# Loading attention keys and queries by halves of the partitions: one transfer of 128 rows becomes two of 64

## The chip, the cores and the metric

The kernel runs on one core of a Trainium2 chip. The core has five engines with instruction streams of their own: TensorE (PE in the profile, with PEld for its weight loads), VectorE (DVE), ScalarE (ACT), GpSimd (POOL) and SyncE (SP), which here only issues transfers. Sixteen DMA engines move data between the off-chip memory and the on-chip buffers. The metric is device time in microseconds (us) of one execution; the time of a kernel is the median of its runs.

## The reference

One layer of a hybrid decoder, for a prompt of 2048 tokens and for 8 sample sequences of 8 tokens. The combined projection feeds two groups of heads: a stick-breaking attention (8 heads of width 64) and a gated DeltaNet (4 heads of width 128). Both outputs go through one output projection and then a gated ConvFFN of width 2816. The part that the change touches is the attention over the prompt:

```python
def sb_block(q, k, v, bias, q_pos, k_pos):
    f32 = jnp.float32
    z = jnp.einsum('bqhd,bkhd->bhqk', q.astype(f32), k.astype(f32)) * (SB_HEAD_DIM ** -0.5)
    z = z + bias.astype(f32)[None, :, None, None]
    mask = k_pos[None, :] < q_pos[:, None]
    log_beta = jax.nn.log_sigmoid(z)
    log_one_minus = jnp.where(mask, jax.nn.log_sigmoid(-z), 0.0)
    later = lax.cumsum(log_one_minus, axis=3, reverse=True) - log_one_minus
    att = jnp.where(mask, jnp.exp(log_beta + later), 0.0)
    out = jnp.einsum('bhqk,bkhd->bqhd', att, v.astype(f32))
    return out.astype(q.dtype)
```

## The kernel before, in words

The program runs through five stages: the modulated norm and the input projection (to about 843 us of the profiled execution), the prompt attention with the DeltaNet recurrence and the sample attention woven into it (843 to about 1716 us), the output projection with the second norm (to about 1962 us), the up-projection with its convolution (to about 2945 us) and the down-projection.

Matmuls get their precision from splitting a number into a rounded part (hi) and a rest (lo). The projection stage writes queries and keys, transposed so that the head dimension is the row, to a buffer `qk_s[2, 2, 512, T]` in the off-chip memory: the first index is query or key, the second is hi or lo, the third is 64 rows for each of the 8 heads, the last is the token.

The attention goes over four pairs of heads `p`, for each over four blocks of 512 query tokens `g`, and inside over the key blocks `c` from `g` down to 0. At the head of a block it loads, all from SP's queue: `ql` (the lo part of both heads' queries, on both halves of the partitions, two transfers of 64 rows, L861), then for each head `e` of the pair a tile `kx` with hi keys in partitions 0 to 63 and lo keys in partitions 64 to 127 (L869) and a tile `q` with the hi queries in both halves (L870), then the values `v` (L874). One matmul then contracts over 128 partitions: (hi keys + lo keys) times hi queries (L892), and a second adds the lo queries (L893). `kx` has nine buffers, `q` four, `ql` two. The tiles are reused from key block to key block, so there are 4 x 4 x 2 = 32 loads of `kx` and as many of `q`, of 128 rows of 2 KB (256 KB) each.

From the scores `z` comes a chain over all engines: a sigmoid on ACT (L894), a mask, one minus it on ACT (L902, L905), the running product on DVE (`P`, L910), a product on DVE, four transposes on PE (`tpa`, L921), a copy on ACT (`aT`, L924) and the matmul with the values on PE (`po`, L929).

Two generators fill the gaps: `delta()`, 17 steps of the recurrence (the function `join` loads `Nm`, L723, and four pieces of `FD`, L727, and inverts a triangular matrix starting at the matmul `qp`, L735; `recur` loads `dT` and `s_`, L777 and L780), and `sample_attention` (the loads `kpg`, L1045, and `vpg`, L1037 and L1046, the matmuls at L1049 to L1091). When the recurrence has ended, the weights of the output projection come in through one buffer `wor` (L1128), split on ACT and DVE into `wo` (L1129, L1130).

The order of the instructions on each engine is not that of the source: a scheduler places the instructions of all engines by its own estimate of their times, once, when the program is built. On the chip each engine then runs its list in that order. SP's list therefore carries loads of all the woven parts, and a row that waits holds up all rows behind it. SP's transfers also take their completion semaphores in turn from a set of eight, and a row waits until the transfer eight rows earlier has landed.

Of the kernel before, what the change touches and what calls it, by code (L numbers as in the profile page):

```python
# [8 lines left out]
F32 = mybir.dt.float32  # L9
# [34 lines left out]
def hybrid_step(  # L44
# [9 lines left out]
    dve, act, pool, pe, sp = nc.vector, nc.scalar, nc.gpsimd, nc.tensor, nc.sync  # L54
# [15 lines left out]
    qk_s = dram.tile([2, 2, 512, T], F32, name="qk_s")  # L70
# [312 lines left out]
    with tc.tile_pool(name="p1a", bufs=1, side="left", reuse_waits="tile") as p1a:  # L383
# [19 lines left out]
        for c2 in range(6):  # L403
            w = split_rows(p1, W[:, 1536 + 256 * c2:1792 + 256 * c2], KD, 256, "w", 10, 6)
            for ci in range(2):
# [3 lines left out]
                for g, (b0, n) in enumerate(GB):  # L409
# [4 lines left out]
                    out = p1a.tile([128, 512], F32, name="dno", tag="dno", bufs=2)  # L414
# [436 lines left out]
    def attention():  # L851
        for p in range(4):
            yield "pair", p
            KS, VS = {}, {}
            for g in range(4):
                gs = slice(512 * g, 512 * g + 512)
# [3 lines left out]
                for x in range(2):  # L860
                    sp.dma_start(out=ql[64 * x:64 * x + 64].bitcast(F32),  # L861
                                 in_=qk_s[0, 1, 128 * p:128 * p + 128, gs].rearrange("(e d) t -> d e t", e=2))
                for e in range(2):
                    h = 2 * p + e
                    hs_ = slice(64 * h, 64 * h + 64)

                    k_ = at_p.tile([128, 512], F32R, name="kx", tag="kx", bufs=9)
                    q = at_p.tile([128, 512], F32R, name="q", tag="q", bufs=4)
                    sp.dma_start(out=k_.bitcast(F32), in_=qk_s[1, :, hs_, gs])  # L869
                    sp.dma_start(out=q.bitcast(F32), in_=qk_s[0, 0, hs_, gs].unsqueeze(0).to_broadcast([2, 64, 512]))  # L870
                    KS[g, e] = k_
                    QS.append(q)
                v = at_p.tile([128, 4, 128], F32, name="v", tag="v", bufs=6)
# [260 lines left out]
    for what, x in attention():  # L1134
        if what == "unit":
            done += 0.55 if x else 1.0
            for f in fill:
                while f[0] is not None and f[2] < f[1] * done / f[3]:
                    f[2] += 1
                    if next(f[0], f) is f:  # L1140
                        f[0] = None
            if fill[0][0] is None and not wos:
                p2.release()
                load_wo("p5wa", 4, 1)
                p5f = tc.alloc_tile_pool(name="p5f", bufs=1, side="left", reuse_waits="tile")
                wpools.append(p5f)
        elif x == 3:
            for f in fill:
                if f[0] is not None:
                    for _ in f[0]:  # L1150
                        pass
            p4.release()
            load_wo("p5wb", 2, 1)
            p5g = tc.alloc_tile_pool(name="p5g", bufs=1, side="left", reuse_waits="tile")
            wpools.append(p5g)
# [458 lines left out]
```

## Time and profile before

| what | value |
|---|---|
| median of 3 runs | 3450.96 us (3447.55 to 3452.15) |
| profiled execution | 3450.76 us, its span 3449.2 us |
| granted TensorE clock, mean | 0.97 |
| PE busy | 3257.8 us, 94% of the span |
| PEld busy | 2749.8 us, 80% |
| DVE busy | 2252.3 us, 65% |
| ACT busy | 1473.0 us, 43% |
| DMA | 460.14 MB, mean 133 GB/s |

The profile's page lists busy time by engine, then the span in 40 slices, the DMA queues, the chain of waits that ended last, and the costliest groups of instructions. A row of the timeline or of the groups names the source line, the engine, and "out<-in" by the names of the tiles; "SPq" is the queue of SP, whose rows are transfers being issued, and their time is that of issuing alone. A row "A <- DMA x" in the list of waits is time that A's engine was idle until a transfer into x had landed. In the table of stretches, "DMA share" is the mean busy share of the sixteen DMA engines.

### The profile page before, as it was taken

To read this page: it belongs to the slowest core of one execution; us is meant where nothing else is said; L and a number is where in the kernel's file an instruction comes from. 1 tells how busy PE (TensorE), PEld (TensorE's weight loads), DVE (VectorE), ACT (ScalarE), POOL (GpSimd) and SP (SyncE) were. 2 spreads that over 40 slices of the span, in tenths; PEclk is the share of its full clock that TensorE was granted. 3 is DMA by queue.
4 is the path that set the end of the run, shared out by engine and by line. 5 is a ranking of instruction groups with operands and counts; after the bars stand their busy time and mean duration, and the time that the engine had idled before them with its cause. 6 is when DMAs were issued, how large, how long until landed. Compare 5 with 4: busy or idle time off the path is not lost.

```text
span 3449.2 us, 54308 instructions
## 1 busy us (share of the span) xinstructions
PE 3257.8 (94%) x19371; PEld 2749.8 (80%) x19371; DVE 2252.3 (65%) x4995; ACT 1473.0 (43%) x3188; POOL 251.8 (7%) x466
## 2 busy tenths in 40 slices
PE   7999999998588998978889999999999999899999
PEld 5968999898355665644578899999999999688887
DVE  5346646876477887879866676666666666656564
ACT  5312336683366785768656632222222222332321
POOL 2000002331011121111100000000000000000000
PEclk9999999999589999989999999999999999999999
DMA  7362239683344555343256532122222222566574
GB/s 238 103 201 83 68 122 276 188 274 95 110 132 126 157 160 159 97 127 105 88 183 193 170 109 69 54 59 59 66 64 60 67 64 63 183 205 205 176 245 132
DMA packets 441996, 460.14 MB, mean 133 GB/s; under 512 B 65543, under 2 KB 343895, under 8 KB 441724
## 3 DMA queue, kind: packets, MB, share of 16 engines
q1 hardware_dynamic: 414012, 411.74, 39.0%
q10 hardware_dynamic: 22080, 28.06, 2.4%
q0 software_dynamic: 5632, 16.86, 1.7%
q8 instruction: 153, 2.51, 0.3%
q14 instruction: 119, 0.97, 0.1%
HBM read 306.56 MB, written 149.97 MB: 132 GB/s over the span
## 4 chain that ended last, share of the span: by engine, by line
PE 81%; DMA 9%; DVE 6%; ACT 2%; issue 2%; SPq 1%; POOL 0%; ACTq 0%; DVEq 0%; POOLq 0%
PE up L229 28%; PE dmm L229 12%; PE fm L229 8%; PE tm L229 7%; PE omm L229 5%; PE po L929 4%; PE tpa L921 3%; PE z L892 2%; DVE P L910 2%; DMA q<-qk_s 2%; PE z L893 1%; DMA wor<-in_w_out_dram 1%; DMA FD<-fd_s 1%; PE mp L204 1%; DMA out_dram<-qkn 1%
## 5 line engine op out<-in xcount | busy, mean ns | idle before, releaser
L229 PE MATMUL up<-sl,wu 128*128 128x424 f32 (+1 forms) x5280 | 1019.2, 355 | 0.0
L229 PEld LDWEIGHTS up<-sl,wu 128*128 128x128 f32 x5280 | 991.0, 188 | 23.9 <-ACT sl L1218 0.4
L229 PE MATMUL dmm<-sl,sl 128*128 128x512 f32 x1848 | 433.3, 395 | 9.5 <-ACT sl L1353 8.3
L229 PEld LDWEIGHTS dmm<-sl,sl 128*128 128x128 f32 x1848 | 347.6, 189 | 94.7 <-ACT sl L1353 11.0
L229 PE MATMUL tm<-w,hh 128*128 128x256 f32 (+1 forms) x2048 | 383.8, 288 | 2.0 <-DVE hh L343 1.4
L910 DVE TENSOR_TENSOR_SCAN P<-P 128x512 f32<-128x512 f32 (+2 forms) x320 | 342.8, 1107 | 44.3 <-ACT P L902 27.3
L229 PEld LDWEIGHTS tm<-w,hh 128*128 128x128 f32 x2048 | 315.1, 190 | 4.0 <-ACT nj L309 1.5
L1428 ACT COPY fpre<-up 128x424 f32<-128x424 f32 (+1 forms) x220 | 110.2, 501 | 481.0 <-PE up L229 481.0
L229 PE MATMUL tm<-w,hl 128*128 128x256 f32 (+1 forms) x1024 | 282.6, 288 | 0.5 <-DVE nr_m L173 0.3
L229 PE MATMUL fm<-hh,w 128*128 128x384 f32 (+2 forms) x960 | 266.9, 357 | 0.0
L894 ACT ACTIVATE sg<-z,bias_b 128x512 f32<-128x512 f32 (+2 forms) x320 | 189.4, 629 | 70.6 <-PE z L893 50.3
L929 PE MATMUL po<-aT,v 128*64 128x512 f32 (+3 forms) x640 | 206.0, 590 | 3.7 <-ACT aT L924 3.7
L924 ACT COPY aT<-tpa 128x512 f32<-128x512 f32 (+1 forms) x320 | 163.9, 529 | 87.4 <-PE tpa L921 64.6
L229 PEld LDWEIGHTS fm<-hh,w 128*128 128x128 f32 x960 | 175.8, 188 | 28.0 <-issue 16.8
L921 PE MATMUL tpa<-ident,sg 128*128 128x128 f32 x1088 | 181.0, 288 | 12.8 <-ACT aT L924 9.9
L921 PEld LDWEIGHTS tpa<-ident,sg 128*128 128x128 f32 x1088 | 128.9, 145 | 79.7 <-issue 33.9
L229 PEld LDWEIGHTS tm<-w,hl 128*128 128x128 f32 x1024 | 188.9, 190 | 1.9 <-DVE hl L344 1.3
L1431 DVE TENSOR_SCALAR fo<-fpre,cwf 128x424 f32<-128x424 f32 (+1 forms) x110 | 47.7, 433 | 214.1 <-ACT fpre L1428 214.1
L892 PE MATMUL z<-kx,q 128*128 128x512 f32 (+2 forms) x320 | 143.9, 451 | 30.1 <-DMA q<-qk_s 26.4
L229 PE MATMUL omm<-wo,mh 128*128 128x512 f32 x512 | 164.2, 400 | 8.0 <-ACT wo L1129 5.1
L229 PE MATMUL fm<-hl,w 128*128 128x384 f32 (+2 forms) x480 | 170.7, 356 | 0.0
L1498 ACT CAST sl<-at 128x1408 fp32r<-128x1408 f32 (+1 forms) x58 | 77.1, 1329 | 202.5 <-PE dmm L229 191.4
(472 smaller groups left out, 5031.2 us busy)
## 6 DMA issues: line engine op xcount, KB each, us to landing
at<-cb_s SPq DMA_DIRECT2D x54, 704.0 KB
wdr<-in_w_down_dram SPq DMA_DIRECT2D x110, 256.0 KB
wada<-in_w_ada_dram SPq DMA_DIRECT2D x48, 512.0 KB
raw<-in_w_up_dram SPq DMA_DIRECT2D x176, 128.0 KB
cb_s<-ff SPq DMA_DIRECT2D x176, 128.0 KB
cb_s<-cb SPq DMA_DIRECT2D x88, 192.0 KB
qk_s<-st SPq DMA_DIRECT2D x128, 128.0 KB
wr<-in_w_in_dram SPq DMA_DIRECT2D x96, 128.0 KB
```

The source lines that it names most:

```text
L204: pe.matmul(mp[32 * c:32 * c + 32, :], lhsT=cT[:, k, :], rhs=wt[:, 512 * c1:512 * c1 + 512], start=(k == 0), stop=(k == KD - 1), tile_posi ...
L229: pe.matmul(out, lhsT=a(k), rhs=b(k), start=(i == 0), stop=(i == 3 * nk - 1))
L892: pe.matmul(z[:, :w], lhsT=QS[e][:, qs_], rhs=KS[c, e][:, :w], start=True, stop=False)
L893: pe.matmul(z[:, :w], lhsT=ql[:, e, qs_], rhs=KS[c, e][:, :w], start=False, stop=True)
L894: act.activation(sg[:, ii, :w], z[:, :w], AF.Sigmoid, bias=bias_b[:, h:h + 1])
L910: dve.tensor_tensor_scan(u, u, u, P[:, ii, w:w + 1], ALU.mult, ALU.bypass)
L921: pe.transpose(tp[:, 128 * i:128 * i + 128], halves[i // 2][:, i % 2, 128 * kb:128 * kb + 128], ident)
L924: act.copy(a_[:, 128 * i0:], tp[:, 128 * i0:])
L929: pe.matmul(po[64 * e:64 * e + 64, c0:], lhsT=VS[c][:, kb, 64 * e:64 * e + 64], rhs=aT[e, kb][:, c0:], start=(diag and kb == 0), stop=(c = ...
L1428: act.copy(pre[:, 2:2 + npr], ps[:, :npr])
L1431: dve.tensor_scalar(out=o[:, :npr], in0=pre[:, 0:npr], scalar1=cwf[:, c, 0:1], scalar2=None, op0=ALU.mult)
L1498: act.copy(ah, raw)
```

## The change

The loads of `kx` and `q` become two transfers each, one for partitions 0 to 63 and one for 64 to 127. For the keys the first half is the hi part and the second the lo part; for the queries both halves read the same hi rows. The bytes, the tiles, the buffers and all arithmetic stay as they were.

```diff
                     k_ = at_p.tile([128, 512], F32R, name="kx", tag="kx", bufs=9)
                     q = at_p.tile([128, 512], F32R, name="q", tag="q", bufs=4)
-                    sp.dma_start(out=k_.bitcast(F32), in_=qk_s[1, :, hs_, gs])
-                    sp.dma_start(out=q.bitcast(F32), in_=qk_s[0, 0, hs_, gs].unsqueeze(0).to_broadcast([2, 64, 512]))
+                    for x in range(2):
+                        sl = slice(64 * x, 64 * x + 64)
+                        sp.dma_start(out=k_[sl].bitcast(F32), in_=qk_s[1, x, hs_, gs])
+                        sp.dma_start(out=q[sl].bitcast(F32), in_=qk_s[0, 0, hs_, gs])
                     KS[g, e] = k_
                     QS.append(q)
```

In the changed program the new transfers stand at L871 and L872, and what stood behind them in the source moves down by two lines. The scheduler, seeing other transfers, also places much of the attention stage in another order, on every engine. Three places on SP's queue show it. The first is the start of the attention: the first block's loads and the first two steps of the recurrence. Before:

```order
L861 DMA ql_10546<-qk_s_60 64x2x512 x2
L869 DMA kx_10549<-qk_s_60 128x1x512
L870 DMA q_10550<-qk_s_60 128x1x512
L869 DMA kx_10553<-qk_s_60 128x1x512
L870 DMA q_10554<-qk_s_60 128x1x512
L874 DMA v_10557<-out_3_dram 128x4x128
L723 DMA Nm_10690<-nm_s_73 128x4x128
L727 DMA FD_10688<-fd_s_74 32x8x32 x4
```

Now:

```order
L861 DMA ql_10546<-qk_s_60 64x2x512 x2
L871 DMA kx_10549<-qk_s_60 64x512
L872 DMA q_10550<-qk_s_60 64x512
L871 DMA kx_10549<-qk_s_60 64x512
L872 DMA q_10550<-qk_s_60 64x512
L871 DMA kx_10555<-qk_s_60 64x512
L872 DMA q_10556<-qk_s_60 64x512
L871 DMA kx_10555<-qk_s_60 64x512
L872 DMA q_10556<-qk_s_60 64x512
L876 DMA v_10561<-out_3_dram 128x4x128
L723 DMA Nm_10694<-nm_s_73 128x4x128
L727 DMA FD_10692<-fd_s_74 32x8x32 x4
```

Here four rows became eight and nothing else moved: `v`, `Nm` and `FD` still stand right behind.

The second place is the third step of the recurrence, where `Nm` and `FD` share the queue with the keys of the fourth query block and the sample attention's first page. Before:

```order
L869 DMA kx_11940<-qk_s_60 128x1x512
L869 DMA kx_11944<-qk_s_60 128x1x512
L1037 DMA vpg_11230<-out_5_dram 8x512
L874 DMA v_11948<-out_3_dram 128x4x128
L723 DMA Nm_11169<-nm_s_73 128x4x128
...
L870 DMA q_11941<-qk_s_60 128x1x512
L940 DMA om_s_67<-ob_10783 128x4x128
...
L869 DMA kx_13037<-qk_s_60 128x1x512
L727 DMA FD_11167<-fd_s_74 32x8x32 x4
```

Now:

```order
L723 DMA Nm_11177<-nm_s_73 128x4x128
L872 DMA q_11292<-qk_s_60 64x512
L871 DMA kx_11297<-qk_s_60 64x512
...
L871 DMA kx_11952<-qk_s_60 64x512
L872 DMA q_11953<-qk_s_60 64x512
L727 DMA FD_11175<-fd_s_74 32x8x32 x4
L871 DMA kx_11952<-qk_s_60 64x512
L872 DMA q_11953<-qk_s_60 64x512
```

`Nm` moved ahead into the loads of the third block, and `FD` stands in the middle of the fourth block's loads, behind the first half of a `q` whose buffer must first come free, and ahead of the sample attention's page, which stood before it.

The third place is where the output projection's weights `wor` come in. Before:

```order
L869 DMA kx_19478<-qk_s_60 128x1x512
L1128 DMA wor_17894<-in_w_out_dram 128x512
...
L1128 DMA wor_17898<-in_w_out_dram 128x512
L870 DMA q_18803<-qk_s_60 128x1x512
L869 DMA kx_19482<-qk_s_60 128x1x512
L1128 DMA wor_17903<-in_w_out_dram 128x512
```

Now:

```order
L871 DMA kx_19140<-qk_s_60 64x512 x2
L849 DMA out_7_dram<-S0_15612 128x8x128
L1130 DMA wor_17942<-in_w_out_dram 128x512
...
L871 DMA kx_19538<-qk_s_60 64x512 x2
L1130 DMA wor_17946<-in_w_out_dram 128x512
L876 DMA v_19550<-out_3_dram 128x4x128
L1130 DMA wor_17951<-in_w_out_dram 128x512
L872 DMA q_18855<-qk_s_60 64x512 x2
```

The weights still alternate with keys and queries; the query load `q_18803`, now in two halves as `q_18855`, stands behind three of them where it stood behind two.

## The prediction

> **What bounds the kernel now.** I read the chain of waits first, since it says which stage can be shortened at all, then the table of stretches over the attention, then the waits of PE and the timeline of SP there.
>
> ```profile
> PE 81%; DMA 9%; DVE 6%; ACT 2%; issue 2%; SPq 1%; POOL 0%; ACTq 0%; DVEq 0%; POOLq 0%
> ...
> core 0: us, PE busy (x) PEld busy (x) DVE busy (x) ACT busy (x) POOL busy (x), PEclk, DMA share, GB/s
> 843.00:960.00 117.00, 55.24 (x330) 37.44 (x329) 41.95 (x82) 33.92 (x76) 6.34 (x31) 0.59 0.36 110
> 960.00:1110.00 150.00, 146.43 (x1107) 95.50 (x1106) 126.28 (x209) 105.29 (x210) 21.19 (x45) 0.94 0.44 126
> 1110.00:1300.00 190.00, 180.25 (x1427) 118.47 (x1425) 160.91 (x249) 138.35 (x286) 39.51 (x73) 0.96 0.52 155
> 1300.00:1345.00 45.00, 33.38 (x279) 22.36 (x278) 30.74 (x64) 24.48 (x60) 3.96 (x21) 0.93 0.57 158
> 1345.00:1490.00 145.00, 141.59 (x1023) 94.09 (x1025) 125.73 (x197) 101.49 (x201) 25.40 (x48) 0.97 0.45 128
> 1490.00:1571.00 81.00, 60.31 (x336) 33.03 (x332) 58.26 (x87) 50.79 (x109) 11.64 (x32) 0.83 0.38 114
> ```
>
> PE ends most of the chain, but 9% of it is waiting for transfers. In the undisturbed stretch from 960 to 1110 us PE is busy 146.4 of 150 us: there TensorE sets the pace, and microseconds that it loses elsewhere in the stage are not caught up. It loses them in three places: 843 to 960 (busy 55 of 117 us, at a clock of 0.59), 1300 to 1345, and 1490 to 1571. What PE waited for, from 843 to 960 (first three rows), from 960 to 1360 (next two) and from 1486 to 1571 (the rest):
>
> ```profile
> PE qp L735 <- DMA FD<-fd_s: 30.1, 2, 28.9
> PE z L892 <- DMA q<-qk_s: 26.4, 3, 12.1
> PE qp L735 <- DMA Nm<-nm_s: 5.2, 1, 5.2
> ...
> PE qp L735 <- DMA FD<-fd_s: 23.5, 3, 10.9
> PE tpp L1049 <- DMA kpg<-in_cache_k_dram: 2.0, 1, 2.0
> ...
> PE tpa L921 <- ACT aT L924: 7.2, 3, 5.8
> PE tpp L1049 <- ACT sgs L1066: 6.9, 1, 6.9
> PE po L929 <- ACT aT L924: 3.7, 1, 3.7
> ```
>
> Only the second row names a tile that the change loads. The others follow from it, which the timeline of SP shows (start, time to issue, row):
>
> ```profile
> 842.67 0.57 SPq L869 DMA_DIRECT2D kx<-qk_s  x1
> 843.36 0.49 SPq L870 DMA_DIRECT2D q<-qk_s  x1
> 843.90 4.75 SPq L869 DMA_DIRECT2D kx<-qk_s  x1
> 848.70 5.48 SPq L870 DMA_DIRECT2D q<-qk_s  x1
> 854.22 5.20 SPq L874 DMA_DIRECT2D v<-out_dram  x1
> 859.52 2.69 SPq L723 DMA_DIRECT2D Nm<-nm_s  x1
> 862.31 5.52 SPq L727 DMA_DIRECT2D FD<-fd_s  x4
> ...
> 921.07 7.14 SPq L869 DMA_DIRECT2D kx<-qk_s  x2
> 928.32 5.19 SPq L1037 DMA_DIRECT2D vpg<-out_dram  x1
> ...
> 944.59 7.48 SPq L727 DMA_DIRECT2D FD<-fd_s  x4
> ```
>
> and two pieces of the chain of waits, whose times run from the issue to the landing:
>
> ```profile
> 843.36 14.16 DMA q<-qk_s
> ...
> 944.59 12.81 DMA FD<-fd_s
> ```
>
> Two transfers of `kx` and `q` go out at 0.5 us each. The third takes 4.75 us to issue, the fourth 5.48, and then even `v`, `Nm` and `FD`, which are other tensors, are held back. The stretches around it say why:
>
> ```profile
> 843.00:845.00 2.00, 2.00 (x19) 2.00 (x19) 0.00 (x0) 0.37 (x1) 0.00 (x0) 1.00 0.91 243
> 850.00:858.00 8.00, 0.34 (x2) 0.38 (x2) 0.00 (x0) 0.00 (x0) 0.00 (x0) 0.55 0.13 48
> ```
>
> From 850 to 858 only `kx` and `q` are in flight: the DMA share is 0.13, which is 2 of 16 engines, and 48 GB/s. A transfer of 256 KB then takes 262144 B / 48 GB/s = 5.46 us, the 5.48 us for which SP hangs. So each of these 64 loads runs on two engines alone, SP's queue is blocked once about two are pending, and all that is queued behind is late. Just before, with `ql`'s two transfers of 64 rows and the first `kx` in flight, the share is 0.91 and the rate 243 GB/s: 64 rows do spread over the engines.
>
> **The change part by part.** It removes 64 issues and adds 128 of half the size.
>
> *The new transfers.* At the rate of the 843 to 845 stretch 128 KB take 131072 / 243 GB/s = 0.54 us; if the halves stayed on two engines, 2.73 us. I take 0.54, because `ql` is the same 64 rows from the same buffer. The issue of one is bounded by these rows (ns, least/median/most):
>
> ```profile
> L1014 SPq DMA_DIRECT2D qsm<-qs_s x1: 503/503/503, 868.6 to 868.6; - x1
> L861 SPq DMA_DIRECT2D ql<-qk_s x32: 585/611/4707, 841.3 to 1577.9; - x32
> L1128 SPq DMA_DIRECT2D wor<-in_w_out_dram x16: 327/342/1376, 1486.7 to 1743.0; - x16
> ```
>
> `qsm` has the very shape of a half (64 rows of 512 numbers): 0.50 us, between 0.34 (`wor`) and 0.61 (`ql`, twice the data). So 128 x 0.50 = 64 us of SP's time stand against 64 x 0.52 = 33 us of unblocked issue before: 31 us more over 860 us, if nothing blocks. In the first block alone the rows from 843.90 to 862.31 take 23.6 us for eight issues that would take 4 unblocked. SP has room, and I charge 5 us for loads that come a few tenths later each (0 to 31).
>
> *843 to 960 us.* PE's waits are 30.1 + 26.4 + 5.2 = 61.7 us. Of the first wait for `q` (12.1 us) some stays: the eight halves are issued from 842.7 at 0.5 us, the first head's four are out by 844.7, and if they land as fast as an undisturbed `wor` does (2.82 us from issue, row below), the matmul starts at 847.0 instead of 843.4 + 14.2 = 857.5. PE was busy until 857.5 - 12.1 = 845.4, so 1.6 us remain. The 28.9 us wait is for an `FD` that was issued at 944.6, behind 7.14 us for `kx`, 5.19 for `vpg` and others; its own issue and landing took 12.8. These go too. But a filling pipeline has waits of its own: undisturbed, 960 to 1110 leaves PE 3.6 us idle in 150, and here the first blocks are short, so I keep 8 us (bounds 2 and 30: the latter if the chain through `qp`, DVE and POOL cannot run faster). Gain 61.7 - 1.6 - 8 = 52. The clock: 330 matmuls in 55.2 us are 167 ns each, against 132 ns in the next stretch, so full clock would give 12 us more; with some idle time left I take 5 (0 to 12).
>
> *960 to 1360 us.* 23.5 + 2.0 = 25.5 us of waits. The last `FD` wait (10.9 us) is this: the chain goes back from the landing, over 5.29 us of transfer, to a queue held by `q` (17.86 us from the start of a blocked `q`):
>
> ```profile
> 1323.10 17.86 DMA q<-qk_s
> 1341.02 5.29 DMA FD<-fd_s
> ...
> 1486.65 8.51 DMA wor<-in_w_out_dram
> ...
> 1504.97 13.68 DMA wor<-in_w_out_dram
> ...
> 1529.41 10.00 DMA wor<-in_w_out_dram
> ...
> 1550.91 2.82 DMA wor<-in_w_out_dram
> ```
>
> The other two waits of that row are alike. I take three quarters: 19 us (10 to 25).
>
> *1486 to 1571 us.* ACT stands at `wo` until `wor` lands and its copies for PE queue behind. Three landings take 8.51, 13.68 and 10.00 us, with `kx` or `q` just ahead of them; the next, alone, takes 2.82. They are late by 32.2 - 8.5 = 23.7 us, of which PE sees 7.2 + 6.9 + 3.7 = 17.8. I take 11 (5 to 17), since the weights still go through one buffer.
>
> Sum: 52 + 5 + 19 + 11 - 5 = 82 us. The profiled execution took 3450.76 us, next to the median of 3450.96; 3450.8 - 82 = 3369 us.
>
> [...]
>
> **The rivals.**
>
> *Something else takes the place (smaller gain).* The recurrence steps form a chain of their own, and the new order puts `FD` behind half a `q` that waits for its buffer. Then only the waits for `q` and `Nm` (26.4 - 1.6 + 5.2 = 30) and the `wor` term (11) go: 41 us, 3410. Against it: those waits end at an `FD` that landed late behind a blocked queue, not at a busy engine. The chance is 0.24.
>
> *All of PE's idle time goes (larger gain).* 61.7 - 1.6 + 12 + 25.5 + 17.8 = 115 us: 3335. It needs a recurrence that never waits, and full clock from the start. The chance is 0.07.
>
> *The halves stay on two engines (the change does not spread them).* The queue is blocked as long as before, the second half of a tile at the same time as the whole was, and 64 more issues at 0.50 us come on top; where SP is blocked they are hidden, elsewhere not: half of 32 us, 3467, slower. It decides as soon as the DMA share under these loads stays near 0.13. `ql` speaks against it. The chance is 0.03.
>
> *Each transfer's fixed part counts (slower).* Of `wor`'s 2.82 us, 2 x 0.54 are data, so 1.74 us are fixed. If SP's queue, with eight transfers pending at most, were bound by that latency, 64 x 1.74 = 111 us would come on top of the gain of 82: 3480. It would need eight pending transfers to take longer to land (2.8 us) than to issue (8 x 0.5 = 4 us), so the rows are against it. [...] The chance is 0.02.
>
> *No change*, by a new order that loses what the loads gain: 0.02.
>
> **How the numbers follow.** The forecast, 3369 us, has a chance of 0.62; alone it spans 3345 to 3395. With the larger part of the smaller-gain case the range is 3340 to 3412, which leaves out the rest of both neighbours and the slow cases. Within 0.2% (7 us) a measurement of this kernel cannot tell a change from none. Faster 0.93, same 0.02, slower 0.05.
>
> **What would show it.** SP's rows for the halves should stay near 0.5 us, with no `v`, `Nm` or `FD` over 3 us for one issue. The DMA share under them should go far above 0.13 in short bursts. PE's waits for `q` should fall from 26.4 to some 2 us and for `FD` before 960 from 30.1 to under 8, the attention should end near 1635 instead of 1716 us, and the stages after it should keep their lengths. Wrong would be: `FD` waits as long as before with a free queue (then the recurrence is the bound), or halves that take 2.7 us each on two engines.

## The result, and the profile after

| | before | changed |
|---|---|---|
| median of 4 runs | 3451.56 us (3447.55 to 3453.89) | 3327.03 us (3320.59 to 3329.44) |
| span of the profiled execution | 3449.2 us | 3324.8 us |

The ratio is 0.9637, with a 95% interval of 0.9621 to 0.9654: the change takes about 125 us off. The forecast was 3369 us with a range of 3340 to 3412, so the direction was right, the gain of 82 us a third too small, and the time below the range. Measured again beside another layout of the buffer ("One transfer of 128 rows again" below), the changed kernel took 3320.0 us against 3449.64 (ratio 0.9626, 0.9613 to 0.9639).

The table of stretches shows where the time went. First the attention as a whole, from the end of the last matmul of the projection to the last matmul with the values, of the kernel before and then of the changed one. The columns are the stretch, its length, the busy time and count of each engine, the granted clock, the DMA share and GB/s:

```profile
845.60:1714.50 868.90, 744.26 (x5355) 471.76 (x5355) 677.51 (x1079) 563.28 (x1150) 131.42 (x305) 0.90 0.42 124
```

```profile
849.90:1596.40 746.50, 716.03 (x5358) 455.71 (x5358) 680.07 (x1086) 564.67 (x1154) 134.40 (x305) 0.98 0.50 146
```

The stage went from 868.9 to 746.5 us, which is 122.4 of the 124.4 us between the two spans. DVE and ACT did the same work in the same busy time; the stages ahead and behind kept their lengths to within 8 us each, and these differences nearly cancel. PE's part splits in two: its idle time fell from 868.9 - 744.3 = 124.6 us to 746.5 - 716.0 = 30.5, a gain of 94, and its busy time fell from 744.3 to 716.0, a gain of 28, for the same matmuls. The clock, 0.90 against 0.98, goes with the second.

The timeline of SP at the start, of the changed kernel, answers to the rows that showed the blocked queue:

```profile
847.04 0.60 SPq L871 DMA_DIRECT2D kx<-qk_s  x1
847.73 0.54 SPq L872 DMA_DIRECT2D q<-qk_s  x1
...
853.77 0.59 SPq L872 DMA_DIRECT2D q<-qk_s  x1
854.41 0.59 SPq L876 DMA_DIRECT2D v<-out_dram  x1
855.10 0.45 SPq L723 DMA_DIRECT2D Nm<-nm_s  x1
855.65 1.93 SPq L727 DMA_DIRECT2D FD<-fd_s  x4
```

None of these rows hangs, though SP stands once, for 2.4 us up to 852.0, until an earlier store has landed. `v` goes out in 0.59 us instead of 5.20, `Nm` in 0.45 instead of 2.69, the four `FD` in 1.93 instead of 5.52. Over all 64 halves of `q` (ns, least/median/most):

```profile
L872 SPq DMA_DIRECT2D q<-qk_s x64: 444/540/1396, 847.7 to 1457.6; - x64
```

Of PE's waits in the attention one for a changed load is left; for `FD` a single wait of 0.4 us remains, further down the list of the changed kernel, whose head is:

```profile
PE tpa L923 <- ACT aT L926: 3.9, 7, 1.4
PE tpt L1085 <- DVE sgs L1076: 3.6, 2, 2.2
PE z L894 <- DMA q<-qk_s: 3.3, 1, 3.3
...
PE qp L735 <- DMA FD<-fd_s: 0.4, 1, 0.4
```

And the first 117 us of the attention, to be read beside the row of 843 to 960 before, and the next stretches:

```profile
849.00:966.00 117.00, 110.20 (x865) 73.73 (x864) 100.66 (x189) 80.65 (x177) 16.16 (x49) 0.90 0.70 190
966.00:1116.00 150.00, 149.78 (x1211) 100.08 (x1209) 137.28 (x224) 116.55 (x243) 25.68 (x62) 1.00 0.54 161
1116.00:1300.00 184.00, 183.96 (x1473) 121.41 (x1475) 164.06 (x259) 139.49 (x288) 35.15 (x77) 1.00 0.53 157
```

PE did 865 matmuls in the time in which it had done 330, and from 966 to 1300 us it idles 0.3 us, at full clock. Most of the idle time that is left lies behind, 23.4 us from 1300 us to the end of the attention.

### The profile page after: what moved, and what is told of

It is laid out like the page before. It is cut to its first block, busy times and chain, and to the rows that moved or that the text cites. A ratio compares the mean times of both kernels' runs of the same rounds, so it can differ in the third digit from the quotient of the medians.

```text
span 3324.8 us, 54372 instructions
## 1 busy us (share of the span) xinstructions
PE 3230.1 (97%) x19371; PEld 2733.8 (82%) x19371; DVE 2250.6 (68%) x4995; ACT 1471.7 (44%) x3188; POOL 255.0 (8%) x466
## 3 DMA queue, kind: packets, MB, share of 16 engines
q1 hardware_dynamic: 415932, 411.75, 40.9%
## 4 chain that ended last, share of the span: by engine, by line
PE 83%; DVE 7%; DMA 6%; ACT 2%; issue 1%; SPq 0%; POOL 0%; ACTq 0%; DVEq 0%; POOLq 0%
PE up L229 28%; PE dmm L229 12%; PE fm L229 8%; PE tm L229 8%; PE omm L229 5%; PE po L931 4%; PE tpa L923 3%; DVE P L912 3%; PE z L894 2%; PE z L895 1%; PE mp L204 1%; DMA raw<-in_w_down_dram 1%; DVE sg L916 1%; DMA nm_s<-Nm 1%; PE tpp L1051 1%
## 5 line engine op out<-in xcount | busy, mean ns | idle before, releaser
L229 PEld LDWEIGHTS up<-sl,wu 128*128 128x128 f32 x5280 | 989.4, 188 | 25.4 <-ACT sl L1220 1.9
L912 DVE TENSOR_TENSOR_SCAN P<-P 128x512 f32<-128x512 f32 (+2 forms) x320 | 343.2, 1108 | 26.4 <-ACT P L907 11.7
L1430 ACT COPY fpre<-up 128x424 f32<-128x424 f32 (+1 forms) x220 | 110.2, 502 | 480.4 <-PE up L229 480.4
L931 PE MATMUL po<-aT,v 128*64 128x512 f32 (+3 forms) x640 | 196.4, 558 | 0.0
```

Source lines behind the costliest of these rows:

```text
L229: pe.matmul(out, lhsT=a(k), rhs=b(k), start=(i == 0), stop=(i == 3 * nk - 1))
L912: dve.tensor_tensor_scan(u, u, u, P[:, ii, w:w + 1], ALU.mult, ALU.bypass)
L931: pe.matmul(po[64 * e:64 * e + 64, c0:], lhsT=VS[c][:, kb, 64 * e:64 * e + 64], rhs=aT[e, kb][:, c0:], start=(diag and kb == 0), stop=(c = ...
L1430: act.copy(pre[:, 2:2 + npr], ps[:, :npr])
```

## The experiments

Theory A: the loads were slow because each ran on two DMA engines, and the gain is their spread over sixteen. Rival B: it is the halving, or the new order of the instructions. Rival C: only the waits of a block's first matmul for its queries count. A further question was where the 28 us of busy time come from.

**The same program with an outermost count of 2, 4 and 8.** The edit keeps the 128 transfers of 64 rows, and every engine's order is row for row that of the changed kernel; only the source's pattern gets an outermost count of 2 (or 4, or 8). The groups of rows overlap, so these kernels load other rows than the changed one and compute other scores, with the same bytes and the same instructions:

```diff
+    spread = lambda a: bass.AP(a.tensor, a.offset, [[16 * T, 2], [T, 32], [1, 512]])
...
-                        sp.dma_start(out=k_[sl].bitcast(F32), in_=qk_s[1, x, hs_, gs])
-                        sp.dma_start(out=q[sl].bitcast(F32), in_=qk_s[0, 0, hs_, gs])
+                        sp.dma_start(out=k_[sl].bitcast(F32), in_=spread(qk_s[1, x, hs_, gs]))
+                        sp.dma_start(out=q[sl].bitcast(F32), in_=spread(qk_s[0, 0, hs_, gs]))
```

> The changed kernel with the same 128 transfers of 64 rows and the same order on every engine, but each transfer's source is read as 2 groups of 32 rows that overlap (rows 0 to 31 and 16 to 47), so that its outermost count is 2. The scores are computed from this other choice of rows. Theory A (the spread over the DMA engines makes the gain): a half takes 128 KB at 48 GB/s = 2.7 us again, SP's queue blocks as before, DMA share 0.13 in the first block, time near the kernel before: 3450 to 3490 us. Rival B (halving or the new order makes the gain): near 3327 us.

> As the run with two groups, but 4 groups of 16 rows (8 rows apart). The scores are computed from this other choice of rows. Theory A: 4 engines, about 96 GB/s, 1.4 us for a half, which is still over twice the 0.55 us that its issue takes: SP still blocks for some time in the first blocks, 3350 to 3400 us. Rival B: near 3327 us.

> As the runs with two and four groups, but 8 groups of 8 rows (4 rows apart). The scores are computed from this other choice of rows. Theory A: 8 engines, about 190 GB/s, 0.7 us for a half, near its issue time of 0.55 us: SP hardly blocks, 3325 to 3340 us.

Measured: a count of 2 takes 3446.33 us (ratio to before 0.9979, 0.9970 to 0.9989); 4 takes 3355.17 (0.9723, 0.9702 to 0.9743); 8 takes 3326.0 (0.9648, 0.9633 to 0.9663). With a count of 2 the timeline of SP hangs again, and a stretch in it has the old share and rate:

```profile
857.86 2.54 SPq L871 DMA_DIRECT2D kx<-qk_s  x1
860.45 2.55 SPq L872 DMA_DIRECT2D q<-qk_s  x1
863.04 2.52 SPq L876 DMA_DIRECT2D v<-out_dram  x1
865.67 2.71 SPq L723 DMA_DIRECT2D Nm<-nm_s  x1
...
855.00:864.00 9.00, 0.00 (x0) 0.00 (x0) 0.00 (x0) 0.00 (x0) 0.00 (x0) 0.54 0.13 48
```

A blocked issue takes 2.5 us, near the time of one 64-row transfer at 48 GB/s (131072 B / 48 GB/s = 2.73 us). With a count of 4, while halves are pending, the share is 0.26:

```profile
850.00:852.00 2.00, 0.00 (x0) 0.00 (x0) 0.43 (x2) 0.75 (x3) 1.86 (x8) 1.00 0.26 95
```

A share of 0.13 is 2 of 16 engines and one of 0.26 is 4 of 16, as the counts of 2 and 4. In the changed kernel, whose halves have a count of 64, the share is 1.01 at 246 GB/s from 848 to 852 us, with the first four halves, `ql` and a store from ACT's queue in flight: all sixteen are busy. For the count of 8 the share is not known; that it puts a half on eight engines is an estimate from the shares of the other two.

So the time follows the outermost count with the program unchanged, and with it the share where it was read: theory A holds, and halving with the new order together give no more than 3452.13 - 3446.33 = 6 us while the loads stay slow. A count of 8 is nearly enough here: a half then takes an estimated 0.7 us, at four times the measured rate of two engines (131072 B / 192 GB/s), near its issue, whose median for `q` is 0.60 us in that run. That eight groups of other rows take the time of the changed kernel also shows that the other rows by themselves cost nothing.

**Keys alone, queries alone.**

```diff
-                        sp.dma_start(out=q[sl].bitcast(F32), in_=qk_s[0, 0, hs_, gs])
+                    sp.dma_start(out=q.bitcast(F32), in_=qk_s[0, 0, hs_, gs].unsqueeze(0).to_broadcast([2, 64, 512]))
```

This is keys alone, the queries whole again; the other run has it the other way round, the keys whole by the line that the change took out.

> Only the key loads are split in halves; the 32 query loads stay whole on two engines. Theory A: half of the slow transfers remain, so a pending pair of queries still delays what is behind it; half of the gain or somewhat more: 3370 to 3400 us. Rival C (it is the wait for the first queries of a block that counts): little gain, over 3410.

> Only the query loads are split; the 32 key loads stay whole on two engines. Theory A: as for keys alone, 3370 to 3400 us. Rival C: most of the gain, under 3350.

Measured: keys alone 3382.41 us (0.9793, 0.9777 to 0.9810), queries alone 3362.99 (0.9744, 0.9727 to 0.9761). The gains, 70 and 89 us, add up to 159, over the 125 of both: either part alone already shortens the same blocked queue. Keys fit theory A. Queries came 7 us under its lower end, but not under the 3350 of rival C, so queries weigh somewhat more and C falls as the whole cause: keys alone also take most of the waits away. What PE still waits for with keys alone (first two rows) and queries alone:

```profile
PE qp L735 <- DMA FD<-fd_s: 18.7, 4, 11.6
PE z L894 <- DMA q<-qk_s: 14.3, 3, 8.5
```

```profile
PE z L894 <- DMA q<-qk_s: 12.4, 2, 8.3
PE qp L735 <- DMA FD<-fd_s: 10.2, 4, 7.2
```

The queries are waited for even when they are spread and only the keys are slow, since SP issues both, and `FD`, which the change never touches, in both cases. These two runs have orders of their own, so how much of the 19 us between them belongs to the loads is not settled.

**Twice as many transfers again.**

```diff
-                    for x in range(2):
-                        sl = slice(64 * x, 64 * x + 64)
-                        sp.dma_start(out=k_[sl].bitcast(F32), in_=qk_s[1, x, hs_, gs])
-                        sp.dma_start(out=q[sl].bitcast(F32), in_=qk_s[0, 0, hs_, gs])
+                    for x in range(4):
+                        sl = slice(32 * x, 32 * x + 32)
+                        hq_ = slice(64 * h + 32 * (x % 2), 64 * h + 32 * (x % 2) + 32)
+                        sp.dma_start(out=k_[sl].bitcast(F32), in_=qk_s[1, x // 2, hq_, gs])
+                        sp.dma_start(out=q[sl].bitcast(F32), in_=qk_s[0, 0, hq_, gs])
```

> Each load in four transfers of 32 rows: 256 transfers in place of 128, on all engines. If the count of transfers costs nothing while TensorE is the bound: 3327 us within 10. If each transfer's issue and fixed part counts: 128 more issues at 0.5 us are 64 us of SP's time, and queued loads come later, 3340 to 3390.

Measured: 3331.83 us, ratio 0.9658 (0.9643 to 0.9672), beside the change's 0.9637 (0.9621 to 0.9654). By these ratios 128 more issues cost some 7 us, with intervals that overlap; beside the second ratio of the changed kernel, 0.9626 (0.9613 to 0.9639), they cost 11 us, and there the intervals do not overlap. Issues at 0.5 us each would be 64 us: SP has room for most of them, and little of an issue or of a transfer's fixed part is on the path. The quarters have an order of their own, which is not separated from this.

**One transfer of 128 rows again, in another layout of the buffer.** The hi and lo row of a head dimension are stored next to each other, so that a load's outermost count is 128 or 64; the lo queries get one transfer for each head in place of one for each half:

```diff
-    qk_s = dram.tile([2, 2, 512, T], F32, name="qk_s")
+    qk_s = dram.tile([2, 512, 2, T], F32, name="qk_s")
...
-                    for x in range(2):
...
+                    sp.dma_start(out=k_.bitcast(F32), in_=qk_s[1, hs_, :, gs].rearrange("d x t -> (d x) t"))
+                    sp.dma_start(out=q.bitcast(F32), in_=qk_s[0, hs_, 0, gs].unsqueeze(1).to_broadcast([64, 2, 512]))
```

> The buffer of queries and keys holds the hi and lo row of one head dimension next to each other, so that each load is one transfer of 128 rows again (64 in place of 128), with an outermost count of 128 or 64. Theory A (the spread alone makes the gain): as fast as the change, 3327 us, or up to 10 us faster for the issues saved. Rival B (halving is what counts): near 3450.

> The changed kernel as it is, beside the layout with hi and lo rows next to each other, on the same chip: 3327 us within 5.

> The layout with hi and lo rows next to each other again. If the 64 issues saved count, or its order is better: 5 to 10 us below the change beside it; if only the spread counts: the same within 3 us.

Measured: 3320.45 us (0.9631, 0.9618 to 0.9644); again, beside the change's 3320.0, 3319.35 (0.9625, 0.9611 to 0.9638). Whole transfers with a count of 128 or 64 are as fast as the halves: rival B falls from this side too. The 64 issues saved give nothing that can be measured, so this is another way to the same time and not a better kernel.

**A gap of TensorE by itself.** Behind all work of the changed kernel, bursts of 64 matmuls with chains of copies on DVE between them:

```diff
+    for n in (1, 2, 4, 8, 12, 16, 24, 32, 48):
+        for e in range(64):
+            gp = pgs.tile([128, 512], F32, name="gp", tag="gp", bufs=2)
+            pe.matmul(gp, lhsT=gi, rhs=gb, start=True, stop=True)
+        gc = pg.tile([128, 512], F32, name="gc", tag="gc", bufs=2)
+        dve.tensor_copy(gc, gp)
+        for e in range(n):
+            dve.tensor_scalar(out=gc, in0=gc, scalar1=1.0, scalar2=0.0, op0=ALU.mult, op1=ALU.add)
+        gb = pg.tile([128, 512], F32R, name="gb", tag="gb", bufs=2)
+        dve.tensor_copy(gb, gc)
```

> The changed kernel with a test stage behind all its work: ten bursts of 64 matmuls (128x128 by 128x512) with a gap of TensorE before each but the first, of 1, 2, 4, 8, 12, 16, 24, 32 and 48 copies on VectorE (some 0.3 to 0.5 us each). Theory (a wait of TensorE costs twice, the wait and a time at half clock behind it): full-clock bursts take 64 x 0.23 = 15 us; behind gaps over some 3 us the granted clock falls to 0.5 for 3.4 to 14 us and the burst takes 2 to 7 us longer, more behind a longer gap. Rival (the clock falls only in a stage of mixed short matmuls, whatever its gaps): all bursts take 15 us.

Measured in one execution. The timeline of PE gives start and length of a burst, and in brackets the gap ahead of it:

```profile
3318.95 19.10 PE L1595 MATMUL gp<-gb,gi 128*128 128x512 f32 x64 [7.86 <-issue]
3339.84 17.99 PE L1595 MATMUL gp<-gb,gi 128*128 128x512 f32 x64 [1.80 <-DVE gb L1601]
3360.10 18.06 PE L1595 MATMUL gp<-gb,gi 128*128 128x512 f32 x64 [2.26 <-DVE gb L1601]
3381.34 19.97 PE L1595 MATMUL gp<-gb,gi 128*128 128x512 f32 x64 [3.18 <-DVE gb L1601]
3406.34 19.64 PE L1595 MATMUL gp<-gb,gi 128*128 128x512 f32 x64 [5.03 <-DVE gb L1601]
3432.85 19.90 PE L1595 MATMUL gp<-gb,gi 128*128 128x512 f32 x64 [6.87 <-DVE gb L1601]
3461.47 19.38 PE L1595 MATMUL gp<-gb,gi 128*128 128x512 f32 x64 [8.72 <-DVE gb L1601]
3493.26 20.26 PE L1595 MATMUL gp<-gb,gi 128*128 128x512 f32 x64 [12.41 <-DVE gb L1601]
3529.63 19.44 PE L1595 MATMUL gp<-gb,gi 128*128 128x512 f32 x64 [16.10 <-DVE gb L1601]
3572.55 20.01 PE L1604 MATMUL gp<-gb,gi 128*128 128x512 f32 x64 [23.48 <-DVE gb L1601]
...
3360.20:3378.10 17.90, 17.90 (x64) 11.70 (x64) 0.00 (x0) 0.00 (x0) 0.00 (x0) 1.00 0.00 0
3381.40:3401.30 19.90, 19.90 (x64) 13.08 (x64) 0.00 (x0) 0.00 (x0) 0.00 (x0) 0.86 0.00 1
3381.40:3386.80 5.40, 5.40 (x13) 3.57 (x13) 0.00 (x0) 0.00 (x0) 0.00 (x0) 0.50 0.01 3
3386.80:3401.30 14.50, 14.50 (x52) 9.51 (x51) 0.00 (x0) 0.00 (x0) 0.00 (x0) 1.00 0.00 0
```

Behind gaps of 1.8 and 2.3 us a burst takes 18.0 us at full clock. From 3.2 us on it takes 19.1 to 20.3: the gap costs its length and 1 to 2 us more. That does not grow with the gap, which the expectation had wrong, as it had the length of a burst at full clock. The last two rows split the burst behind the gap of 3.2 us: its first 5.4 us run at a granted clock of 0.50 with 13 matmuls, some 415 ns each, the rest at 1.00 with some 279 ns each. So about a third of the busy time at half clock is lost in this burst, not half. A gap of 3.2 us was enough here, and the half clock reached 5.4 us into the burst. In the attention of the kernel before, the shortest gap with the start of a half clock in it is 3.15 us, up to 1073.8 us, and the stretches at half clock last 3.4 to 17.1 us, but for the two longest, of 68.2 and 37.5 us.

**The busy time.** The runs with counts of 2, 4 and 8 have the order of the changed kernel, so the busy time of PE over the same matmuls can be compared directly. The row of the attention for 2, 4 and 8:

```profile
851.50:1716.10 864.60, 746.69 (x5359) 471.79 (x5358) 682.42 (x1086) 564.97 (x1154) 131.21 (x305) 0.91 0.44 126
```

```profile
849.80:1619.60 769.80, 723.62 (x5359) 460.40 (x5358) 680.53 (x1086) 564.59 (x1154) 131.41 (x305) 0.97 0.50 142
```

```profile
851.00:1598.40 747.40, 715.37 (x5358) 455.37 (x5358) 680.21 (x1086) 564.76 (x1155) 133.99 (x305) 0.98 0.51 146
```

With 2, PE idles 864.6 - 746.7 = 117.9 us and is busy 746.7 at a clock of 0.91; with 4, 46.2 and 723.6 at 0.97; with 8, 32.0 and 715.4 at 0.98. The order is the same, so the 31 us of busy time between the counts of 2 and 8 are no matter of order: they come and go with the waits and the clock.

The granted clock itself tells how much of it is the clock. In the attention every stretch is at 0.50 or at 1.00. The nine stretches at 0.50 of the kernel before (the two longest and the sum of all), then the two of the changed kernel (the longer and the sum):

```profile
850.80:919.00 68.20, 40.63 (x233) 26.46 (x234) 26.07 (x58) 22.81 (x54) 1.28 (x12) 0.50 0.32 98
932.70:970.20 37.50, 12.56 (x68) 7.11 (x69) 6.50 (x10) 4.01 (x9) 0.13 (x2) 0.50 0.50 145
...
sum 170.50, PE 94.11 PEld 52.94 DVE 60.23 ACT 53.18 POOL 1.83; mean PE 10.46 PEld 5.88 DVE 6.69 ACT 5.91 POOL 0.20
...
852.10:876.00 23.90, 22.02 (x122) 14.93 (x123) 16.99 (x39) 14.11 (x34) 0.66 (x10) 0.50 0.75 212
...
sum 27.30, PE 25.42 PEld 16.78 DVE 18.32 ACT 15.63 POOL 0.66; mean PE 12.71 PEld 8.39 DVE 9.16 ACT 7.81 POOL 0.33
```

PE is busy for 94.1 us at half clock before and for 25.4 now, 68.7 us less. If a third of that is loss, as in the burst above, it is worth an estimated 23 us, and 34 if it is half; the 28 us measured lie between. The half clock can thus account for all of the 28 us; what share of each shape's time it takes is not measured.

## Why the prediction was wrong, point by point

*Two engines, and a blocked queue behind them*: right. The run on two engines gives the old time back with everything else as changed.

*The new transfers, 0.50 us of issue each, 0.54 us of data*: right as to the issue, with a median of 0.54 us and no blocked rows at the start. The 5 us charged for later loads were not there: 64 whole loads with an outermost count of 128 or 64 take the same time as 128 halves (3319.35 against 3320.0 us).

*843 to 960 us, 52 us of idle time*: nearly right. PE idled 117.0 - 55.2 = 61.8 us in that stretch and 117.0 - 110.2 = 6.8 in the first 117 us now, which is 55 less. The first wait is 3.3 us rather than 1.6, as the half that ends it landed 4.1 us after its issue and not 2.82.

*The clock, 5 us, between 0 and 12*: this is the step that failed. I priced it from the mean of the matmuls in the first stretch alone, 167 against 132 ns. Those are mixed shapes, and the first blocks have more of the narrow ones. The other disturbed stretches, among them the two whose rows showed clocks of 0.93 and 0.83, I put at nothing. Measured are 28 us between before and changed, and 31 us with the order held fixed. The rows of half clock show where they were: the first two stretches, up to 970 us, held 40.6 + 12.6 = 53.2 of the 94.1 us of busy time at half clock, and the seven later ones the other 40.9. Of the first part the changed kernel still has 22.0 us, so it gives 31 of the 68.7 us; the later ones give 37, more than the stretch that I priced. The clocks quoted in the prediction would have said so: with a clock of c over a length L and only full and half speed, 2 x (1 - c) x L us are at half clock, which is 2 x 0.41 x 117 = 96 us for the first stretch.

The waits bring this clock about: the timeline of PE has eleven gaps of more than 3 us in the attention before and one now, and eight of the nine stretches of half clock before begin inside one of them. The ninth, 1567.6 to 1571.0 us, begins behind a gap of only 1.5 us and a shorter one, so the step seen between 2.3 and 3.2 us holds for a single gap between dense bursts and not for every place in the kernel.

*960 to 1360 us, 19 of 25.5 us*: the mechanism was right and the size a quarter too small. PE idled 400.0 - 373.6 = 26.4 us there. Of the `FD` waits 0.4 us is left in the whole attention, and PE idles 0.3 us from 966 to 1300.

*1486 to 1571 us, 11 us*: right in kind. The chain of the changed kernel has these landings of `wor`, against 8.51, 13.68 and 10.00 before:

```profile
1398.02 3.01 DMA wor<-in_w_out_dram
1417.36 4.11 DMA wor<-in_w_out_dram
1429.34 3.75 DMA wor<-in_w_out_dram
```

They are hardly late now, against 2.82 us for the one that was alone. Their gain cannot be taken alone from the two traces, since the end of the attention is woven differently now; what the two earlier stretches leave of the 94 us of idle time, 94 - 55 - 26 = 13 us, is an estimate of it.

*The sum*: idle time forecast at 52 + 19 + 11 - 5 = 77 us, measured 94; clock forecast at 5, measured 28. Of the 40 us missed in the stage, 23 are the clock and 17 are idle time: some 3 in the first stretch, 7 in the second, 2 at the end, and the 5 charged for later loads. Most of that I had held back for a recurrence that would wait by itself. It hardly does: with transfers in time, PE's waits for it (`qp`, L735, and `vp`, L807) come to about 1 us. The rival "all of PE's idle time goes" (3335 us) was the nearest, with a chance of 0.07, and even it had the clock at 12 and came out above the measured time. The rivals on the other side fell: the new order costs nothing (at most 6 us gained, together with the halving), the halves do spread (a DMA share of 1.01 from 848 to 852 us), and little of a transfer's fixed part is on the path. For the last of these, the ratios of halves, quarters and whole loads with a count of 128 or 64 lie within 0.4% of each other.

## What to carry to other kernels

Look at the outermost count of the source's pattern of a transfer, not at its bytes alone: in this kernel a leading dimension of two, hi and lo or a repeated source, put 256 KB on two of sixteen engines (a share of 0.13, 48 GB/s). The sign in the profile was a DMA share near k/16 with little else in flight, 0.13 for a count k of 2 and 0.26 for 4, and long issue rows of transfers that have nothing to do with the slow ones, such as 5.20 us for `v`; the waits then name those other tiles. A wait of TensorE that brings the granted clock down is to be priced with its clock: its own length, and a third to a half of the busy time that then falls at a clock of 0.50. In this kernel that was 28 us for 69 us of such time, a quarter of the gain.

## What the runs showed of the hardware that was not expected

The price of a single gap between dense bursts is a step: nothing at 2.3 us, 1 to 2 us from 3.2 to 23.5 us alike. A burst at a granted clock of 0.50 is not twice as slow: its matmuls started every 415 ns against 279. And an outermost count of 8 is nearly as good as one of 64 for these loads (ratios of 0.9648 against 0.9637 and 0.9626, so 4 to 8 us, with intervals that overlap), while a count of 4 still costs 28 us, though a half on four engines lasts only an estimated 1.4 us at their rate of 95 GB/s.
